# Eight dummy matmuls, a new order of the set-up block and one weight made by an accumulating transfer, in a causal convolution by nested differences

## Chip, cores, metric

The kernel runs on one core of one Trainium2 chip. The metric is the device time of one execution in microseconds (us). Before the change it was 780.17 us (median of three, 780.01 to 780.49). A ratio is the mean of a kernel's runs over the mean of the runs of before in the same rounds, so it is not quite the ratio of the medians that are quoted.

## The reference

A causal convolution of eight taps, each a 512 x 512 matrix:

```python
out = np.zeros_like(x)                      # x: 8 x 4096 x 512, kernel: 8 x 512 x 512
for k in range(8):
    shifted = x if k == 0 else np.concatenate([np.zeros((B, k, D)), x[:, :-k, :]], axis=1)
    out += np.matmul(shifted, kernel[k])
```

## The kernel before

Time is cut into 128 runs of 256 steps, one run to a partition, and eight steps make a group. Inside a group the eight taps are applied by three nested levels of a multiplication-saving scheme: sums of x (tiles `D4`, `D42`, `D421`, ...) meet 8 loaded weights and 19 differences of weights (index `MID`). A **node** is one third of a group: nine products of four 512-column matmuls each. The steady loop runs the nodes with TensorE gapless. What the change touches is the set-up block before it, in which the taps land, the first x is transposed by TensorE, node 0 is computed by 16 plain products (`direct`), and VectorE makes the 19 differences. Each engine runs its own instructions in the order of the text; waits between engines follow from the tiles they share.

```python
def fill(pw):                                # a pair of dummy matmuls on zeros
    for h in range(2):
        nc.tensor.matmul(pw[:, h], lhsT=zero[:, 0:P], rhs=zero, start=True, stop=True)

def product(bank, comp, w, start):           # four 128x512 matmuls
    for c in range(DC):
        nc.tensor.matmul(bank, lhsT=comp[:, c * P:(c + 1) * P], rhs=w[:, c, :], ...)

def mid_dve(*which):                         # one weight difference on VectorE
    o, u, v = mid(*which)
    tt(o, u, v, SUB)

def node_a1(k):  ...  # product into q[:, 1]; ScalarE copies it to q[:, 0]
def node_a0(n):       # product onto q[:, 0]
def node_u(n):        # product onto q[:, 1]: must wait for that copy
def node_seed(n, b_): # ScalarE copies q[:, 1] to the bank where the node's v product adds
def node_dts(n):      # ScalarE copies q[:, 0] to SBUF
def node_d(n, b_):    # VectorE: correction from dts and v
# ... cut ...
    direct(3, 0)
    fill(pair(2))
    direct(3, 1)
    tt(D41[:, 1], T4[:, 0], T4[:, 1], ADD)
    load_w(3)
    node_a1(1)
    node_u(nodes[1])
# ... cut ...
    node_a0(nodes[3])
    node_e(nodes[2], 0)
    prep_d42(HI)
    node_l(nodes[2], 1, LO)
    node_u(nodes[3])
    node_seed(nodes[3], 0)
    node_l(nodes[2], 1, HI)
    mid_dve(0, HI, LO)
    node_seed(nodes[3], 1)
```

## Time and profile before

| | before |
|---|---|
| span of the profiled execution | 778.4 us |
| TensorE busy | 765.6 us, 98% |
| VectorE busy | 658.7 us, 85% |
| first product starts | 11.78 us |
| x transposes (first work that needs the second load of x) start | 24.51 us |
| TensorE gapless from | 60.67 us |
| TensorE's waits from 24.5 to 61 us, summed | 2.8 us |

Read such a profile from its end: the chain that ended last says which engine set each stretch. The share of busy time hides that the first 61 us and the rest have different limits. A matmul's own line gives the idle time before it in brackets, and what ended it; for a wait that a pipelined engine can hide in its queue, the distance from start to start is the better measure, 216 ns where nothing waits.

### The profile page before, as it was taken

To read this page: it belongs to the slowest core of one execution; us is meant where nothing else is said; L and a number is where in the kernel's file an instruction comes from. 1 tells how busy PE (TensorE), PEld (TensorE's weight loads), DVE (VectorE), ACT (ScalarE), POOL (GpSimd) and SP (SyncE) were. 2 spreads that over 40 slices of the span, in tenths; PEclk is the share of its full clock that TensorE was granted. 3 is DMA by queue.
4 is the path that set the end of the run, shared out by engine and by line. 5 is a ranking of instruction groups with operands and counts; after the bars stand their busy time and mean duration, and the time that the engine had idled before them with its cause. 6 is when DMAs were issued, how large, how long until landed. Compare 5 with 4: busy or idle time off the path is not lost.

```text
span 778.4 us, 9432 instructions
## 1 busy us (share of the span) xinstructions
PE 765.6 (98%) x3576; PEld 346.9 (45%) x3576; DVE 658.7 (85%) x767; ACT 282.7 (36%) x461; POOL 41.2 (5%) x79
## 2 busy tenths in 40 slices
PE   6999999999999999999999999999999999999997
PEld 3444444444444444444444444444444444444443
DVE  4999988898888898888898888898888898878895
ACT  3453343333343333343333343333343333343332
POOL 4000000000000000000000000000000000000000
PEclk9999999999999999999999999999999999999999
DMA  9975887877787878787787687877797867687843
GB/s 198 211 125 137 214 198 181 194 166 185 166 177 194 195 166 177 171 194 179 175 189 183 166 202 170 195 168 185 166 192 176 204 162 185 167 181 184 205 132 122
DMA packets 159229, 138.90 MB, mean 178 GB/s; under 512 B 130128, under 2 KB 134224, under 8 KB 159056
## 3 DMA queue, kind: packets, MB, share of 16 engines
q1 hardware_dynamic: 145456, 99.89, 46.0%
q0 software_dynamic: 13584, 38.15, 31.1%
q8 instruction: 28, 0.46, 0.2%
q10 hardware_dynamic: 144, 0.26, 0.1%
q14 instruction: 17, 0.14, 0.1%
HBM read 77.33 MB, written 67.11 MB: 186 GB/s over the span
## 4 chain that ended last, share of the span: by engine, by line
PE 92%; DVE 4%; DMA 2%; issue 1%; POOL 1%; DVEq 0%; ACT 0%; ACTq 0%; POOLq 0%
PE pp L190 92%; DMA xin<-in_x_dram 2%; DVE w L76 2%; DVE D L76 1%; POOL w L80 0%; DVE pp L76 0%; DVE pp L265 0%; DVE XT L383 0%; PE pp L179 0%; DVE y L76 0%; DVE A L76 0%; POOL xin L80 0%; DVEq L635 0%; ACT pp L249 0%; POOL XT L80 0%
## 5 line engine op out<-in xcount | busy, mean ns | idle before, releaser
L190 PE MATMUL pp<-w,D 128*128 128x512 bf16 x3280 | 716.8, 379 | 4.2 <-DMA w<-in_kernel_dram 2.6
L190 PEld LDWEIGHTS <-D 128*128 128x128 bf16 x3280 | 320.4, 98 | 392.8 <-issue 3.3
L76 DVE TENSOR_TENSOR D<-D 128x1024 bf16<-128x1024 bf16 (+1 forms) x252 | 228.4, 945 | 1.0 <-ACT D L346 0.9
L76 DVE TENSOR_TENSOR y<-pp,ms 128x1024 f32<-128x1024 f32 (+1 forms) x121 | 146.2, 1211 | 45.4 <-PE pp L190 45.4
L76 DVE TENSOR_TENSOR D<-XT 128x2048 bf16<-128x2048 bf16 (+2 forms) x153 | 142.3, 945 | 11.2 <-DMA XT<-xin 9.2
L237 ACT COPY pp<-pp 128x512 f32<-128x512 f32 x95 | 54.1, 570 | 255.1 <-PE pp L190 255.0
L249 ACT COPY pp<-pp 128x512 f32<-128x512 f32 x95 | 54.2, 570 | 172.2 <-PE pp L190 170.0
L76 DVE TENSOR_TENSOR pp<-dts,pp 128x512 f32<-128x512 f32 x95 | 65.5, 689 | 43.9 <-ACT dts L255 42.6
L292 ACT COPY ms<-pp 128x1024 f32<-128x1024 f32 x60 | 61.0, 1016 | 33.0 <-PE pp L190 33.0
L80 POOL DMA_DIRECT2D xin<-in_x_dram x64 | 34.0, 532 | 687.2 <-DMA XT<-xin 672.6
L265 DVE SCALAR_TENSOR_TENSOR pp<-pp,dts 128x512 f32<-128x512 f32 x95 | 65.8, 693 | 3.3
L255 ACT COPY dts<-pp 128x512 f32<-128x512 f32 x95 | 57.5, 606 | 2.0 <-PE pp L190 2.0
L251 ACT ACTIVATE pp<-pp 128x512 f32<-128x512 f32 x95 | 56.1, 590 | 0.8 <-DVE y L76 0.8
L190 PE MATMUL pp<-w,XT 128*128 128x512 bf16 x120 | 30.8, 379 | 0.0
L76 DVE TENSOR_TENSOR w<-w,w 128x2048 bf16<-128x2048 bf16 x19 | 22.8, 1217 | 0.3 <-DMA w<-in_kernel_dram 0.2
L190 PEld LDWEIGHTS <-XT 128*128 128x128 bf16 x120 | 11.7, 98 | 14.2
L190 PE MATMUL pp<-w,w 128*128 128x512 bf16 x36 | 9.2, 378 | 1.3 <-ACT pp L237 0.7
L190 PE MATMUL pp<-w,F 128*128 128x512 bf16 x36 | 8.9, 379 | 0.0
L391 ACT COPY XT<-pp 128x1024 bf16<-128x1024 bf16 x1 | 1.0, 1012 | 17.5 <-PE pp L179 17.5
L173 PE MATMUL pp<-zero 128*128 128x512 bf16 x16 | 6.1, 539 | 1.2 <-DVE zero L145 1.2
L331 DVE MEMSET D<- 128x64 bf16 x2 | 0.2, 112 | 7.9 <-ACT D L343 7.7
L80 POOL DMA_DIRECT2D w<-in_kernel_dram x8 | 6.0, 755 | 4.1 <-DMA w<-in_kernel_dram 3.0
(53 smaller groups left out, 69.9 us busy)
## 6 DMA issues: line engine op xcount, KB each, us to landing
out_dram<-y SPq DMA_DIRECT2D x123, 512.0 KB, 3.5
xin<-in_x_dram POOLq DMA_DIRECT2D x64, 512.0 KB, 5.8
w<-in_kernel_dram POOLq DMA_DIRECT2D x8, 512.0 KB, 17.5
D<-in_x_dram SPq DMA_DIRECT2D x1, 1024.0 KB, 4.9
out_dram<-ms SPq DMA_DIRECT2D x2, 512.0 KB, 3.2
out_dram<-f SPq DMA_DIRECT2D x2, 512.0 KB, 4.3
XT<-xin SPq DMA_TRANSPOSE x61, 6.1
XT<-in_x_dram POOLq DMA_DIRECT2D x1, 384.0 KB, 10.9
```

What stands on the lines that cost most here:

```text
L76: nc.vector.tensor_tensor(out=o, in0=a, in1=b, op=op)
L80: nc.gpsimd.dma_start(out=out, in_=src)
L173: nc.tensor.matmul(pw[:, h], lhsT=zero[:, 0:P], rhs=zero, start=True, stop=True)
L190: nc.tensor.matmul(bank, lhsT=comp[:, c * P:(c + 1) * P], rhs=w[:, c, :], start=start and c == 0, stop=c == DC - 1, skip_group_check=True)
L237: nc.scalar.copy(out=n.q[:, 0], in_=n.q[:, 1])
L249: nc.scalar.copy(out=n.p[b_][:, 1], in_=n.q[:, 1])
L251: nc.scalar.mul(out=n.p[b_][:, 1], in_=n.q[:, 1], mul=-1.0)
L255: nc.scalar.copy(out=n.dts, in_=n.q[:, 0])
L265: nc.vector.scalar_tensor_tensor(out=p[:, 0], in0=p[:, 1], scalar=-1.0, in1=n.dts, op0=MUL, op1=SUB)
L292: nc.scalar.copy(out=ms[b_], in_=p)
L331: nc.vector.memset(z[:, :, 0:D:G], 0.0)
L391: nc.scalar.copy(out=XT[:, 0:2], in_=bank["x2"][:, 0:2])
```

## The change

Its stated intent: keep TensorE's clock up while the first tap is on its way, fit the order of the set-up to measured landings, and take one weight difference off VectorE: ScalarE writes the negated weight and a transfer adds the other one to it.

```diff
+    def mid_neg(u, v):
+        nc.scalar.mul(out=W[MID, u, v], in_=W[LO, u, v], mul=-1.0)
+
+    def mid_acc(u, v):
+        nc.gpsimd.dma_start(out=W[MID, u, v], in_=W[HI, u, v], accum_op=ADD)
 ...
     transpose_pe("h1", 0, H, 6, 8)
+    fill(pair(2))
     nc.scalar.copy(out=to(XF[:, 0:2]), in_=prev(bank["h0"]))
-    first_run(XF[:, 0:2])
     transpose_pe("x0", 2, xin[0, 0], 0, 2)
     nc.scalar.copy(out=XF[:, 4:6], in_=bank["x0"])
+    nc.scalar.copy(out=to(XF[:, 2:4]), in_=prev(bank["h1"]))
+    fill(pair(2))
+    first_run(XF[:, 0:2])
     tt(D4[:, 0:2], XF[:, 0:2], XF[:, 4:6], ADD)
+    fill(pair(2))
     load_w(5)
-    transpose_pe("xb", 3, xin[0, 0], 2, 4)
+    transpose_pe("xb", 0, xin[0, 0], 2, 4)
 ...
     tt(D2, XF[:, 1:6], XF[:, 3:8], ADD)
+    fill(pair(2))
 ...
     mid_dve(2, LO, MID)
+    mid_neg(HI, LO)
 ...
     prep_d421(HI)
-    mid_dve(0, HI, HI)
+    mid_acc(HI, LO)
 ...
     node_a0(nodes[3])
+    tt(D21[:, 0:2], C0[:, 0:2], C1[:, 0:2], ADD)
+    node_u(nodes[3])
     node_e(nodes[2], 0)
     prep_d42(HI)
+    mid_dve(0, LO, HI)
     node_l(nodes[2], 1, LO)
-    node_u(nodes[3])
     node_seed(nodes[3], 0)
     node_l(nodes[2], 1, HI)
-    mid_dve(0, HI, LO)
     node_seed(nodes[3], 1)
-    tt(D421[:, 0:4], D42[:, 3:7], D42[:, 4:8], ADD)
+    node_dts(nodes[3])
+    node_v(nodes[3], 1)
 ... (lines are left out within the hunks too; some sixty more move by a few places. The operations added or removed are the four `fill`s, the negation and the transfer, and `mid_dve(0, HI, LO)`; `xb` changes its bank; everything else that stands here with one sign moves)
```

More of the change, by code (lines that the diff above doesn't have):

```diff
@@ L342 @@
     transpose_pe("h1", 0, H, 6, 8)
+    fill(pair(2))
     nc.scalar.copy(out=to(XF[:, 0:2]), in_=prev(bank["h0"]))
-    first_run(XF[:, 0:2])
     transpose_pe("x0", 2, xin[0, 0], 0, 2)
     nc.scalar.copy(out=XF[:, 4:6], in_=bank["x0"])
+    nc.scalar.copy(out=to(XF[:, 2:4]), in_=prev(bank["h1"]))
+    fill(pair(2))
+    first_run(XF[:, 0:2])
     tt(D4[:, 0:2], XF[:, 0:2], XF[:, 4:6], ADD)
+    fill(pair(2))
     load_w(5)
-    transpose_pe("xb", 3, xin[0, 0], 2, 4)
-    nc.scalar.copy(out=to(XF[:, 2:4]), in_=prev(bank["h1"]))
-    direct(0, 0)
-    nc.vector.tensor_copy(out=XF[:, 6:8], in_=bank["xb"])
+    transpose_pe("xb", 0, xin[0, 0], 2, 4)
     first_run(XF[:, 2:4])
     fill(pair(3))
+    direct(0, 0)
     transpose_pe("he", 1, H, 1, 4)
-    tt(D4[:, 2:4], XF[:, 2:4], XF[:, 6:8], ADD)
     load_w(7)
     load_x(0, 1)
+    nc.vector.tensor_copy(out=XF[:, 6:8], in_=bank["xb"])
     tt(D2, XF[:, 1:6], XF[:, 3:8], ADD)
+    fill(pair(2))
+    tt(D4[:, 2:4], XF[:, 2:4], XF[:, 6:8], ADD)
+    load_x(1, 0)
     direct(0, 2)
+    tt(to(E4[:, 1:4]), prev(bank["he"]), to(XF[:, 1:4]), ADD)
+    load_w(2)
+    direct(2, 2)
     direct(0, 3)
-    load_x(1, 0)
-    tt(to(E4[:, 1:4]), prev(bank["he"]), to(XF[:, 1:4]), ADD)
-    direct(2, 2)
+    direct(0, 1)
     nc.vector.tensor_copy(out=F0, in_=XF[:, 4])
-    direct(0, 1)
-    first_run(E4[:, 1:4])
     direct(1, 1)
@@ L370 @@
     mid_dve(1, LO, HI)
+    first_run(E4[:, 1:4])
     mid_dve(2, LO, HI)
+    load_w(0)
+    direct(2, 0)
     tt(F21, D2[:, 0:4], D2[:, 1:5], ADD)
-    direct(2, 0)
+    direct(2, 3)
     mid_dve(2, LO, LO)
-    load_w(2)
     mid_dve(1, LO, LO)
-    load_w(0)
     direct(1, 3)
-    direct(2, 3)
     mid_dve(2, LO, MID)
+    mid_neg(HI, LO)
     direct(1, 0)
@@ L385 @@
     direct(1, 2)
+    nc.scalar.copy(out=C0[:, 0:2], in_=XT[:, 6:8])
+    prep_d42(HI)
     tt(D42[:, 3], D4[:, 1], D4[:, 3], ADD)
@@ L393 @@
     nc.scalar.copy(out=XT[:, 2:4], in_=bank["x2"][:, 2:4])
-    nc.scalar.copy(out=C0[:, 0:2], in_=XT[:, 6:8])
     nc.scalar.copy(out=C1, in_=XT[:, 0:4])
-    prep_d42(HI)
     tt(T4, XT[:, 4:8], XT[:, 0:4], ADD)
     direct(3, 0)
-    fill(pair(2))
     direct(3, 1)
     tt(D41[:, 1], T4[:, 0], T4[:, 1], ADD)
-    load_w(3)
+    fill(pair(2))
     node_a1(1)
-    node_u(nodes[1])
     tt(D41[:, 0], D4[:, 7], T4[:, 0], ADD)
     tt(T42[:, 0:2], D4[:, 6:8], T4[:, 0:2], ADD)
+    load_w(3)
     tt(D421[:, 0], D42[:, 7], T42[:, 0], ADD)
@@ L409 @@
     mid_dve(1, HI, HI)
-    load_w(1)
+    node_u(nodes[1])
     node_e(nodes[0], 0)
-    load_x(1, 1)
-    load_x(2, 0)
     prep_d27()
     mid_dve(2, HI, LO)
+    load_w(1)
     node_a0(nodes[1])
+    load_x(1, 1)
     node_seed(nodes[1], 0)
@@ L419 @@
     node_dts(nodes[1])
+    load_x(2, 0)
     tt(D421[:, 1:4], T42[:, 0:3], T42[:, 1:4], ADD)
+    load_x(2, 1)
     node_d(nodes[1], 0)
@@ L423 @@
     mid_dve(1, HI, LO)
+    node_v(nodes[1], 1)
+    mid_dve(2, HI, HI)
+    mid_dve(2, HI, MID)
     node_e(nodes[0], 1)
-    mid_dve(2, HI, HI)
-    node_v(nodes[1], 1)
-    mid_dve(2, HI, MID)
     node_l(nodes[1], 0, HI)
-    load_x(2, 1)
     node_d(nodes[1], 1)
     prep_d421(HI)
-    mid_dve(0, HI, HI)
+    mid_acc(HI, LO)
     node_a1(2)
@@ L435 @@
     node_e(nodes[1], 0)
+    mid_dve(0, HI, HI)
     transpose_x(1, 1)
@@ L438 @@
     node_u(nodes[2])
+    prep_d4(HI)
     node_l(nodes[1], 1, LO)
-    node_seed(nodes[2], 0)
-    prep_d4(HI)
     nc.scalar.copy(out=D4[:, 2:4], in_=T4[:, 2:4])
@@ L444 @@
     node_seed(nodes[2], 1)
+    node_seed(nodes[2], 0)
     node_dts(nodes[2])
     node_v(nodes[2], 0)
+    node_e(nodes[1], 1)
     node_d(nodes[2], 0)
-    node_e(nodes[1], 1)
     node_v(nodes[2], 1)
-    node_l(nodes[2], 0, HI)
     nc.scalar.copy(out=D42[:, 3], in_=T42[:, 3])
@@ L454 @@
     nc.scalar.copy(out=U1, in_=XT[:, 0])
+    node_l(nodes[2], 0, HI)
     node_a1(3)
@@ L458 @@
     node_a0(nodes[3])
+    tt(D21[:, 0:2], C0[:, 0:2], C1[:, 0:2], ADD)
+    node_u(nodes[3])
     node_e(nodes[2], 0)
     prep_d42(HI)
+    mid_dve(0, LO, HI)
     node_l(nodes[2], 1, LO)
-    node_u(nodes[3])
     node_seed(nodes[3], 0)
     node_l(nodes[2], 1, HI)
-    mid_dve(0, HI, LO)
     node_seed(nodes[3], 1)
-    tt(D421[:, 0:4], D42[:, 3:7], D42[:, 4:8], ADD)
+    node_dts(nodes[3])
+    node_v(nodes[3], 1)
     node_e(nodes[2], 1)
-    node_dts(nodes[3])
-    mid_dve(0, LO, HI)
-    node_v(nodes[3], 1)
     tt(A1[:, 0], C0[:, 1], C1[:, 0], ADD)
     mid_dve(1, MID, HI)
+    tt(D421[:, 0:4], D42[:, 3:7], D42[:, 4:8], ADD)
     node_v(nodes[3], 0)
@@ L481 @@
     node_a0(nodes[4])
-    node_l(nodes[3], 0, HI)
     node_dts(nodes[4])
@@ L486 @@
     tt(A1[:, 1], C1[:, 0], C1[:, 1], ADD)
-    load_x(3, 0)
-    tt(D21[:, 0:2], C0[:, 0:2], C1[:, 0:2], ADD)
     transpose_x(2, 0)
     mid_dve(2, MID, LO)
+    node_l(nodes[3], 0, HI)
     node_e(nodes[3], 0)
@@ L496 @@
     node_seed(nodes[4], 1)
+    node_e(nodes[3], 1)
     node_v(nodes[4], 0)
-    node_e(nodes[3], 1)
     node_d(nodes[4], 0)
+    node_v(nodes[4], 1)
     node_a1(5)
-    node_v(nodes[4], 1)
     node_l(nodes[4], 0, HI)
@@ L505 @@
     prep_m()
-    node_a0(nodes[5])
-    node_seed(nodes[5], 0)
     node_d(nodes[4], 1)
     node_y(nodes[4], 0, LO)
+    node_l(nodes[4], 1, LO)
     tt(F21[:, 0], D2[:, 0], D21[:, 0], ADD)
     node_y(nodes[4], 0, HI)
-    node_l(nodes[4], 1, LO)
+    node_a0(nodes[5])
+    load_x(3, 0)
     prep_d4(LO)
+    node_seed(nodes[5], 0)
     node_l(nodes[4], 1, HI)
@@ L516 @@
     node_v(nodes[5], 0)
-    store(0, LO, 0, first[0, LO, 0])
+    prep_d27()
     node_seed(nodes[5], 1)
     node_y(nodes[4], 1, LO)
-    prep_d27()
     node_d(nodes[5], 0)
     node_v(nodes[5], 1)
+    node_a1(6)
+    tt(F21[:, 1], D21[:, 0], D21[:, 1], ADD)
+    store(0, LO, 0, first[0, LO, 0])
     node_d(nodes[5], 1)
     store(0, HI, 0, first[0, HI, 0])
-    tt(F21[:, 1], D21[:, 0], D21[:, 1], ADD)
+    load_x(3, 1)
     node_y(nodes[4], 1, HI)
-    node_a1(6)
     node_l(nodes[5], 0, LO)
     node_a0(nodes[6])
-    load_x(3, 1)
     transpose_x(2, 1)
@@ L536 @@
     prep_d41(LO)
-    node_y(nodes[5], 0, HI)
+    node_l(nodes[5], 1, HI)
     node_l(nodes[5], 1, LO)
@@ L540 @@
     store(0, HI, 1, first[0, HI, 1])
+    node_y(nodes[5], 0, HI)
     node_y(nodes[5], 0, LO)
+    node_seed(nodes[6], 1)
+    tt(D21[:, 0:2], D2[:, 0:2], D2[:, 1:3], ADD)
     node_v(nodes[6], 0)
-    node_l(nodes[5], 1, HI)
+    node_y(nodes[5], 1, HI)
+    node_dts(nodes[6])
     store(1, LO, 0, first[1, LO, 0])
-    node_dts(nodes[6])
+    node_d(nodes[6], 0)
+    node_y(nodes[5], 1, LO)
+    node_v(nodes[6], 1)
+    node_d(nodes[6], 1)
     store(1, HI, 0, first[1, HI, 0])
-    tt(D21[:, 0:2], D2[:, 0:2], D2[:, 1:3], ADD)
-    node_d(nodes[6], 0)
-    node_y(nodes[5], 1, HI)
-    node_y(nodes[5], 1, LO)
-    node_seed(nodes[6], 1)
-    node_v(nodes[6], 1)
     tt(D21[:, 2:4], D2[:, 2:4], D2[:, 3:5], ADD)
-    node_d(nodes[6], 1)
     prep_d42(LO)
     store(1, HI, 1, first[1, HI, 1])
-    node_a1(7)
     prep_d4(HI)
     store(1, LO, 1, first[1, LO, 1])
+    node_a1(7)
     for k, (i, a) in enumerate(order):
```

## The prediction

> **What bounds the kernel now.** I read the page's busy table first, then the chain that ended last, then a table of stretches, then each engine's timeline of the first 62 us.
>
> ```profile
> PE 765.6 (98%) x3576; PEld 346.9 (45%) x3576; DVE 658.7 (85%) x767; ACT 282.7 (36%) x461; POOL 41.2 (5%) x79
> ...
> PE pp L190 92%; DMA xin<-in_x_dram 2%; DVE w L76 2%; DVE D L76 1%; POOL w L80 0%; DVE pp L76 0%; DVE pp L265 0%; DVE XT L383 0%; PE pp L179 0%; DVE y L76 0%; DVE A L76 0%; POOL xin L80 0%; DVEq L635 0%; ACT pp L249 0%; POOL XT L80 0%
> ```
>
> TensorE is the bound: 98% busy, 92% of the chain. The source has 16 products in the set-up block and 9 for each of 95 nodes, 871 in all, each of four 512-column matmuls: 3484. Their median spacing in the trace is 216 ns, so they need 3484 x 0.216 = 752.5 us of the 778.4 us span. No part of the change removes one. What it can win is time in which TensorE waits before it becomes gapless. When is that?
>
> ```profile
> 5.94 18.53 DMA xin<-in_x_dram
> ...
> 24.51 1.08 PE pp L179 x16
> ...
> 59.39 1.24 DVE w L76
> 60.63 0.05 issue
> 60.67 169.66 PE pp L190 x784
> ```
>
> This is the chain in order of time (start, us, what). It has three parts: until 24.46 us it waits for a load of x, queued since 5.94 us; from 25.6 to 60.6 us it runs through VectorE without a break; from 60.67 us TensorE is gapless. Everything the change touches is in the first two parts, and 717 us of the span are out of its reach.
>
> ```profile
> 8.30:11.70 3.40, 0.92 (x17) 0.74 (x14) 1.76 (x5) 2.17 (x3) 1.29 (x2) 0.97 1.17 197
> 11.70:15.10 3.40, 3.32 (x16) 1.68 (x17) 1.84 (x2) 0.00 (x0) 1.49 (x2) 0.53 1.12 186
> ...
> 15.20:18.50 3.30, 2.25 (x14) 1.06 (x12) 2.99 (x5) 0.00 (x0) 0.74 (x1) 1.00 1.23 201
> ```
>
> The stretches' columns are length, busy time of TensorE, its weight loads, VectorE, ScalarE and GpSimd, the granted clock, the DMA share and GB/s. TensorE works 0.92 us in the first stretch, and in the next its clock is 0.53. That is what the dummy matmuls are to cure.
>
> The remaining waits, from TensorE's timeline:
>
> ```profile
> 11.78 1.87 PE L190 MATMUL pp<-w,D 128*128 128x512 bf16 x4 [2.56 <-DMA w<-in_kernel_dram]
> ...
> 16.47 4.48 PE L190 MATMUL pp<-w,D 128*128 128x512 bf16 x20 [1.05 <-DVE w L76]
> ...
> 33.63 1.02 PE L190 MATMUL pp<-w,w 128*128 128x512 bf16 x4 [0.66 <-ACT pp L237]
> ...
> 36.18 2.02 PE L190 MATMUL pp<-w,w 128*128 128x512 bf16 x8 [0.66 <-ACT pp L249]
> ...
> 52.63 6.27 PE L190 MATMUL pp<-w,D 128*128 128x512 bf16 x28 [0.35 <-ACT pp L251]
> ```
>
> I measured each wait as the start-to-start distance of neighbours less 0.216 us. After 24.5 us: 0.82 at 33.63, 0.82 at 36.18, 0.13 at 37.17, 0.23 at 46.06, 0.51 at 52.63, 0.05 at 54.41, 0.21 at 60.67. Sum 2.8 us. All later ones add to about 0.5 us. So even a perfect set-up after 24.5 us would win 2.8 us, 0.4% of the time.
>
> **What the Trainium skill says.** (1) "TensorE: Matmul & The Clock Gate", Part 1: an idle array falls to half clock, judged in free-running windows of 3.4 us. The trace agrees: 3.4 us at about half clock after the nearly idle stretch, with 427 ns between matmuls (12.16 to 12.59 us) in place of 216. (2) Same page, Part 4: transposes do not count as busy in the same way. The trace fits: the 17 transposes in the first stretch did not hold the clock; it does not separate this from plain idleness. (3) "DMA: Bandwidth & Descriptors", section "SWDGE vs HWDGE vs iDMA": an accumulating transfer can only be issued by GpSimd, so the new one shares that queue with the x loads. (4) Same page, "Two DMAs through the same engine are not ordered": a queue's transfers start in order. The trace's landings agree: the loads issued between 1.9 and 28.5 us land in order of issue, mostly 2.5 us apart (taps 4, 6, 5, 7 at 11.64, 16.13, 18.67, 21.22; x at 24.46 and 26.56; taps 2, 0, 3, 1 at 29.10, 31.64, 34.19, 36.74; x at 39.18 and 41.66).
>
> **Part 1: dummy matmuls and the new order before 24.5 us.** The change adds four pairs of dummies (8 matmuls, 8 x 0.216 = 1.7 us warm). Three pairs stand before the first product, one before the second; all in time that was idle or cold. I walked the new order by hand. ScalarE's first three copies stay about 1 us each but the middle two shift, VectorE copies x's second half at about 11.8 (0.7 us), and the first product now also waits for that copy because it takes over its PSUM bank: start about 12.6, later than 11.78, but warm, so it ends near 13.5 as before. The H transposes (landing 13.54) end near 14.3; VectorE does the 5-row and 2-row adds, then the add into E4 ends near 15.6, which frees the bank for the second product: 15.6 against 16.47. Nine products follow, 9 x 0.864 = 7.8 us, ending at 23.4 against 24.24. The next work in both orders is the transposes of the x that lands at 24.46, and the same ten products stand before it in both. **The 0.9 us gained is therefore waited away there.** The order of loads is the same in both, and the queue never runs dry, so the landing stays. Worth: 0.0; only an execution with a badly placed clock window (0.27 us of slack in before) could show more.
>
> **Part 2: 24.5 to 38 us.** The same products, transposes and one dummy pair stand in the same order (the pair moves behind one product). The two 0.82 us waits are a product that must wait for ScalarE to read the bank it will write; the order around both is unchanged. Worth: 0.
>
> **Part 3: the weight made by DMA, and the order from 38 to 61 us.** ScalarE negates one weight (2048 columns; a copy of that size took 1.91 us) in time when it idles, so that is free. VectorE loses one 1.22 us subtraction, 1.14 us of its pitch, which stood at 49.39 us. A 1,024-column add moved ahead of the third node's gives 0.60 back until 56 us:
>
> ```profile
> 51.51 0.57 ACT L249 COPY pp<-pp 128x512 f32<-128x512 f32 x1 [1.64 <-PE pp L190]
> 51.99 0.59 ACT L251 ACTIVATE pp<-pp 128x512 f32<-128x512 f32 x1
> ...
> 54.27 0.69 DVE L265 SCALAR_TENSOR_TENSOR pp<-pp,dts 128x512 f32<-128x512 f32 x1
> ```
>
> The 0.51 us wait at 52.63 is a product waiting for these two ScalarE seeds, which wait for the product before. That product (the u of node 3) moves one place earlier, so two products (1.73 us) cover the 1.1 us of seeds in place of one: the wait goes. Then VectorE must keep up: its correction of node 3 moves from 54.27 to 54.27 - 1.14 + 0.60 = 53.7 and ends at 54.4, for a product at 54.7; the last two mid weights end 1.1 us earlier, near 59.4 and 60.5, for products near 59.9 and 60.8. The 0.21 goes too. The 0.23 at 46.06 stays, since the VectorE operations ahead of it are the same and one waits for a transposed x (landed 43.74). Sum: 0.51 + 0.21 + 0.05 = **0.75 us**.
>
> **Rivals.** (a) **The accumulating transfer lands late.** It is issued after the x load that went out at 44.26, so about 45; that load's data ended near 48.7 and landed at 50.97. Estimate for the add: 2.5 to 3 us of data like a load, then a landing up to 2.3 us after, so 52 to 54. The subtraction that reads it now stands at 55.47 - 1.14 + 0.60 = 54.9 in VectorE's order, and its result is needed near 56.4. A landing at 57 would cost 57 + 1.2 - 56.4 = 1.8 us: the kernel would take about 781.2. For it: no transfer of this kind is in the trace, and transposes use the engines from 49 to 52.6 us. Against it: the order is said to be fitted to measured landings. I give it a third. (b) **The warm clock is worth its face value**: the 3.4 cold us bring 1 us or more, and the result is near 778.5. For it: the cold stretch is real. Against it: the 24.46 landing. (c) **New waits** in the reordered nodes 4 to 6, where before had none: up to 0.5 us slower, 780.3.
>
> **Range and chances.** 780.17 - 0.75 = 779.4 with the transfer in time; a third of a chance of something like +0.3 us from it moves the middle to 779.5. The low end takes rival (b) in full, the high end a transfer about 1.5 us too late. The executions of before spread by 0.48 us, which is inside the range. All of it is far inside 2% (15.6 us): 98 to 99% within, 1% faster, under 1% slower.
>
> **What would show it.** In the changed profile: the granted clock near 1.0 from 11.7 to 15.1 us (the dummies did their work), the second product about 0.9 us earlier, and yet the x transposes still starting within 0.1 us of 24.5; the waits near 33.6 and 36.2 still there with 0.66; the one near 52.6 gone; VectorE without a wait for a DMA near 55 us; TensorE's gapless part starting with the same work about 0.7 us earlier. The prediction is wrong if the x transposes start well before 24.4, if a load lands at another time, or if VectorE waits for the accumulated weight.

## The result, and the profile after

779.5 us (median of four, 779.29 to 779.61) against 780.09 us for before in the same rounds: ratio 0.9992, 95% interval 0.9974 to 1.0009. By this interval it is "the same". All four executions lie below all four of before, and in the second measurement (below) four of five lie below all nine, so a small gain is likely; how large it is, the times don't settle. The traces can say more, because they show each wait.

The page of the changed kernel, busy time and chain by line:

```profile
PE 766.8 (99%) x3584; PEld 347.3 (45%) x3584; DVE 657.5 (85%) x766; ACT 284.9 (37%) x462; POOL 42.3 (5%) x80
...
PE pp L197 96%; DMA xin<-in_x_dram 2%; POOL w L80 0%; PE pp L186 0%; ACT y L295 0%; DVE y L76 0%; DVE pp L76 0%; POOL xin L80 0%; DVEq L647 0%; ACT pp L256 0%; ACT pp L244 0%; POOL XT L80 0%; PE pp L180 0%; POOL ident masks.py:199 0%; POOL ident masks.py:197 0%
```

The eight dummies make TensorE look 1.2 us busier, and the span is 1.1 us shorter all the same: busy time of a dummy is not work. VectorE has one instruction less. Its lines of weights have left the chain, and TensorE's share rose from 92 to 96%. The chain in order of time:

```profile
5.96 18.30 DMA xin<-in_x_dram
...
24.31 1.07 PE pp L186 x16
...
45.14 0.69 DVE pp L76
45.83 0.04 issue
45.87 726.95 PE pp L197 x3364
```

It still waits for the same load of x, landed at 24.26 us (24.46 before). But the 35 us through VectorE are gone from it: VectorE still has as much to do, but its last step on this chain is the correction that ends at 45.83 us. The stretches, columns as in the prediction:

```profile
8.30:11.70 3.40, 2.19 (x17) 1.04 (x15) 0.83 (x3) 2.20 (x3) 0.00 (x0) 1.00 1.17 193
11.70:15.10 3.40, 3.05 (x29) 1.71 (x27) 2.89 (x5) 0.00 (x0) 2.57 (x4) 1.00 1.15 187
...
15.20:18.50 3.30, 2.49 (x12) 1.20 (x13) 2.92 (x6) 0.09 (x1) 0.86 (x2) 1.00 1.23 203
```

The clock is 1.00 where it was 0.53. One trace doesn't show that the dummies did it, since windows fall differently in each execution; but over all profiles, none of the six with the added dummies has a cold (half-clock) window between 8 and 30 us, and six of the eight without them have one or two (most of these versions are described below). TensorE's timeline, start and length in us, idle time before in brackets:

```profile
13.01 1.02 PE L197 MATMUL pp<-w,D 128*128 128x512 bf16 x4 [0.35 <-DVE D L367]
...
16.01 4.48 PE L197 MATMUL pp<-w,D 128*128 128x512 bf16 x20 [0.88 <-DVE w L76]
...
24.31 1.07 PE L186 MATMUL pp<-ident,xin 128*128 128x128 bf16 x16 [0.37 <-DMA xin<-in_x_dram]
...
33.44 1.02 PE L197 MATMUL pp<-w,w 128*128 128x512 bf16 x4 [0.66 <-ACT pp L244]
...
35.98 2.02 PE L197 MATMUL pp<-w,w 128*128 128x512 bf16 x8 [0.66 <-ACT pp L256]
37.87 20.26 PE L197 MATMUL pp<-w,D 128*128 128x512 bf16 x92
```

The second product starts 0.46 us earlier, and then the x transposes wait for their load. The two waits of 0.66 us are where they were. From 37.87 us on 92 matmuls follow with no wait in the listing where before had one at 52.63 us.

The account of the 1.08 us by which the last matmul starts earlier (772.43 against 773.51 us): the load of x landed 0.20 us earlier; the waits from 24.3 to 62 us sum to 2.2 in place of 2.8 us (0.78 to 0.14 between 50 and 62 us); the small waits after 62 us sum to about 0.25 us less. Only the middle item, 0.6 us, is the change's by the argument of the prediction. The medians differ by 0.59 us.

One measure takes out the landing of x: the time from the start of the x transposes to the start of the last matmul. It is 749.00 to 749.45 us in six profiles with the old order (before, and the variants of it below) and 748.02 to 748.65 us in six with the new order (the changed kernel twice, its variants without dummies, and the short load). The two groups do not overlap, though single late waits of 0.3 to 0.7 us stand in both.

### The profile page after: what moved, and what is told of

Its sections match the earlier page's. It is cut to its first block, busy times and chain, and to the rows that moved or that the text cites. A ratio compares the mean times of both kernels' runs of the same rounds, so it can differ in the third digit from the quotient of the medians.

```text
span 777.3 us, 9450 instructions
## 1 busy us (share of the span) xinstructions
PE 766.8 (99%) x3584; PEld 347.3 (45%) x3584; DVE 657.5 (85%) x766; ACT 284.9 (37%) x462; POOL 42.3 (5%) x80
## 4 chain that ended last, share of the span: by engine, by line
PE 96%; DMA 2%; POOL 1%; ACT 0%; issue 0%; DVE 0%; DVEq 0%; POOLq 0%
PE pp L197 96%; DMA xin<-in_x_dram 2%; POOL w L80 0%; PE pp L186 0%; ACT y L295 0%; DVE y L76 0%; DVE pp L76 0%; POOL xin L80 0%; DVEq L647 0%; ACT pp L256 0%; ACT pp L244 0%; POOL XT L80 0%; PE pp L180 0%; POOL ident masks.py:199 0%; POOL ident masks.py:197 0%
## 5 line engine op out<-in xcount | busy, mean ns | idle before, releaser
L180 PE MATMUL pp<-zero 128*128 128x512 bf16 x24 | 8.9, 505 | 2.4 <-DVE zero L145 1.2
L197 PEld LDWEIGHTS <-w 128*128 128x128 bf16 x36 | 3.5, 97 | 5.8 <-issue 2.1
```

## The experiments

My theory: the load of x that lands near 24.3 us sets the start of what follows, so nothing done before it counts; the gain is that ScalarE's seeds of node 3 and VectorE's last weights no longer make TensorE wait between 50 and 62 us, and both had to go together. Rivals: the warm clock is worth its face value; or VectorE's saved subtraction is.

### The dummies alone

To the kernel before I added the four pairs only, at the same places (after the `h1` transposes, two after the copy of `x0`, one after the add into `D2`).

> The kernel before with nothing but the four added pairs of dummy matmuls. My theory (the x load that lands near 24.3 to 24.5 us sets the start of everything after it): the clock stays near 1.0 from 11.7 to 15.1 us, the second product starts about 1 us earlier (near 15.4 in place of 16.47), TensorE then idles about 1.3 us before the x transposes, which still start within 0.05 us of that load's landing; time within 0.2 us of before, so 780.0 to 780.3. Rival (the warm clock is worth its face value): about 1 us faster, near 779.1.

Measured: 781.05 us against 780.48 us, ratio 1.0004 (0.9992 to 1.0017): no gain. The median is above the 780.0 to 780.3 that I had said: the profiled execution took 780.48 us, the four others 780.83 to 781.17, and no trace shows why. From the stretches and TensorE's timeline of this run:

```profile
11.70:15.10 3.40, 2.85 (x27) 1.71 (x26) 2.74 (x4) 0.00 (x0) 2.68 (x4) 1.00 1.14 192
```

```profile
16.19 4.48 PE L190 MATMUL pp<-w,D 128*128 128x512 bf16 x20 [1.58 <-DVE w L76]
...
24.49 0.68 PE L179 MATMUL pp<-ident,xin 128*128 128x128 bf16 x9 [0.38 <-DMA xin<-in_x_dram]
```

The clock is full, and the x transposes start at 24.49 us, where the load landed at 24.45. My figure for the second product was wrong: 16.19, not 15.4, because in the old text order the dummies wait for a ScalarE copy and hold up the transposes behind them. It made no difference, which is the point. The waits from 24.5 to 62 us equal those of before. The rival's 1 us is not there.

### The changed kernel without the dummies

> The changed kernel without the four added pairs of dummies, its order kept. My theory: the clock falls to a half somewhere between 11.7 and 16 us, the first product and the H transposes run at half rate, the second product starts near 16.8 in place of 16.01, the ten products end near 24.6 in place of 23.6, so at most 0.3 us of it passes the load's landing at 24.3: 779.5 to 779.8. Rival (warm clock worth its face value): 1 us or more slower than the changed kernel, 780.5 or above.

Measured: 780.18 us against 780.48 us for before, ratio 0.9997 (0.9983 to 1.0010). In its trace one clock window is cold (from 12.0 to 15.4 us), the second product starts at 16.20, the x transposes at 24.37 with the load landed at 24.32, and the waits to 62 us sum to 2.07 us: the set-up is as good as with the dummies. But TensorE waited 0.67 us near 386 us, far from anything changed. The median stood above my range; that wait explains it for the profiled execution alone. I ran the kernel again, below.

### The u product alone, the transfer alone, both

The first variant of before:

```diff
     node_a0(nodes[3])
+    node_u(nodes[3])
     node_e(nodes[2], 0)
     prep_d42(HI)
     node_l(nodes[2], 1, LO)
-    node_u(nodes[3])
```

> The kernel before with only the u product of node 3 moved one place earlier, which in the changed kernel covers the two ScalarE seeds. My theory: the 0.51 us wait near 52.6 goes, but VectorE, whose list is unchanged and without a gap to 60.6 us, does not get earlier, so TensorE waits about as long a little later (near 54.7 for the correction of node 3 that ends at 54.96, and near 60.7 for the mid weight): gapless part starts at 60.67 as before; time 780.0 to 780.2. Rival (the wait is worth its own length wherever it is removed): 0.5 us faster, 779.6.

The second replaces `mid_dve(0, HI, LO)` in before by `mid_neg` and `mid_acc`, at the changed kernel's places:

> The kernel before with only the weight by negation and accumulating transfer in place of one VectorE subtraction. My theory: VectorE is about 1.1 us earlier from 49.4 us on, waits up to 0.6 us for the transfer (landing near 54.9 as in the changed kernel), the 0.51 us wait near 52.6 stays because ScalarE's seeds make it, the 0.21 us at 60.67 goes: 0.2 to 0.3 us faster, 779.8 to 779.9. Rival (the freed 1.14 us of VectorE is worth itself): 1.1 us faster, 779.0.

The third does both:

> The kernel before with both: the u product of node 3 one place earlier and the weight by negation and accumulating transfer. My theory (the two waits guard one another: ScalarE's seeds at 52.6 us, VectorE's list from 54 to 60.7 us): the waits between 50 and 62 us, 0.78 us in before, 0.78 with the first part alone and 0.55 with the second alone, fall to 0.1 to 0.2 us, so 0.6 to 0.7 us faster than before, which is the whole gain of the changed kernel without its dummies and without its new front. Rival (effects add): 0 plus 0.23 us, so 0.55 us of waits stay.

| kernel | median us | before us | ratio (95% interval) | waits in its trace, 50 to 62 us |
|---|---|---|---|---|
| before | | | | 0.52 + 0.05 + 0.21 = 0.78 us |
| u product alone | 780.15 | 780.48 | 0.9999 (0.9986 to 1.0011) | 0.57 + 0.21 = 0.78 |
| transfer alone | 780.36 | 780.48 | 1.0002 (0.9989 to 1.0014) | 0.51 + 0.04 = 0.55 |
| both | 780.59 | 780.60 | 1.0005 (0.9992 to 1.0017) | 0.35 |
| changed kernel | 779.50 | 780.09 | 0.9992 (0.9974 to 1.0009) | 0.14 |

None of the four ratios is clear of 1, and the times of the transfer alone and of both missed what I had said (779.8 to 779.9, and 0.6 to 0.7 us faster). The waits are read from one profile each; before's 0.78 us came out the same in the profiles of the dummies alone and of the short load. The waits of the first two are as expected: moving the product alone moves the wait 2 us on, to a product that needs a weight from VectorE (I had expected it to wait for the correction):

```profile
55.26 4.49 PE L190 MATMUL pp<-w,D 128*128 128x512 bf16 x19 [0.40 <-DVE w L76]
```

(That execution runs 0.9 us late, see the next part, so 55.26 is 54.4 of before.) The two together take out 0.43 us, where I had said 0.6 to 0.7. What is left shows in VectorE's timelines, the first line from the kernel with both, the second with the transfer alone:

```profile
54.33 0.70 DVE L271 SCALAR_TENSOR_TENSOR pp<-pp,dts 128x512 f32<-128x512 f32 x1 [0.44 <-ACT dts L261]
```

```profile
54.14 0.70 DVE L271 SCALAR_TENSOR_TENSOR pp<-pp,dts 128x512 f32<-128x512 f32 x1 [0.61 <-ACT dts L261]
```

VectorE now waits for node 3's `dts`, a ScalarE copy that stands behind a 1 us copy of node 2's result in the old order. The changed kernel puts it ahead of that copy (the last `+` lines of the diff above), which I had not counted as a part of its own. So the two together are not the whole gain. That `dts` is the **third** part is argued and not tested by a run of its own: the changed kernel also moves a 1,024-column add (0.60 us of VectorE) out of this stretch, which might cover the 0.35 us by itself.

The time of the variant with both shows none of its 0.43 us: its load of x landed at 24.95, 0.5 us later than before's, and it had the 0.7 us wait near 387 us too (the transfer alone had 0.58 us there). Executions differ by as much as the whole gain.

### What the clock costs when it falls for longer

The profile of the u product alone happened to fall on an execution with two cold windows in a row (12.7 to 19.5 us); from its stretches and its TensorE timeline:

```profile
12.70:19.50 6.80, 5.23 (x22) 2.62 (x22) 5.05 (x7) 0.00 (x0) 1.48 (x2) 0.50 1.23 203
```

```profile
25.38 1.06 PE L179 MATMUL pp<-ident,xin 128*128 128x128 bf16 x16
```

The load had landed at 24.35 us, yet the transposes start at 25.38, right behind the product before: here TensorE itself is late. This execution has a mean clock of 0.994. This kernel's two executions at 0.994 took 781.10 and 780.93 us, its three at 1.0 took 780.06 to 780.15: two cold windows cost 0.9 us. One alone costs nothing (before's own profile has one, and its x transposes start 0.05 us after the landing), so this is the price of the second. Over all runs with the old beginning (before and its variants without the added dummies), 6 of 46 executions of which I have the clock were at 0.994. With the dummies (the changed kernel twice, and the short load below) none of 13 was under 0.999. If the dummies prevent it, they are worth 0.9 us in one execution in eight, about 0.1 us in the mean, and nothing in the median. That it is they is not shown: the 15 executions of the new order without dummies (below) had none at 0.994 either, the lowest being one at 0.995. The prediction had this only as a half sentence ("an execution with a badly placed clock window").

### Taking the landing away

Both kernels with a quarter of tap 7 loaded and the rest zeros, so that the x load behind it lands earlier. Their outputs are wrong, which doesn't matter for the times.

```diff
-    load_w(7)
+    w7 = W[LO, LO, LO]
+    load(w7[:, 0:1], kr[:, 0:1, 7, :])
+    for c in range(1, DC):
+        nc.scalar.copy(out=w7[:, c], in_=zero)
```

> Wrong result on purpose: the kernel before, but only a quarter of tap 7 is loaded (the rest is zeros written by ScalarE), so that the load of x behind it lands about 1.9 us earlier, near 22.5 us. My theory: TensorE reaches the x transposes when its ten products are done, near 24.25 us, in place of 24.5, so they start at most 0.3 us earlier and the time falls by 0.2 to 0.3 us; in an execution whose clock falls to a half for two windows nothing is won. Rival (the landing isn't what binds): no change in both kernels.

> Wrong result on purpose: the changed kernel with the same quarter of tap 7. My theory: its ten products are done near 23.6 us, so the x transposes now start near 23.6 in place of 24.3 and the time falls by about 0.7 us against the changed kernel; the part of the front's gain that the landing hid comes out. Rival (the landing isn't what binds): no change.

The load landed at 22.12 us in the one and 21.62 us in the other. The x transposes, in before and in the changed kernel:

```profile
23.36 1.06 PE L179 MATMUL pp<-ident,xin 128*128 128x128 bf16 x16
```

```profile
23.75 1.06 PE L186 MATMUL pp<-ident,xin 128*128 128x128 bf16 x16
```

Now nothing waits for the load, and both start right behind their ten products: 1.15 us earlier in the variant of before, 0.56 us in that of the changed kernel. Times: 779.59 us for the first (three executions at 779.54 to 779.62, one at a clock of 0.994 at 781.20) and 778.77 us for the second, against 780.60 us for before: ratios 0.9994 (0.9980 to 1.0008) and 0.9980 (0.9964 to 0.9995), the second alone clear of 1. The theory that this landing binds holds by the traces, and the times agree: with it out of the way both kernels gain about 1 and 0.7 to 0.8 us (the second against the changed kernel's 779.5, from other rounds). That before gained more than I had said has a plain reason: this profile fell on an execution with no cold window at all, so its products, from 11.36 us on, ran warm. The old beginning with a warm clock is in fact 0.4 us quicker through its ten products than the new one, whose first product waits for a VectorE copy until 13.01 us; only the landing hides it. (The profile of the transfer alone, warm by chance too, shows the same: second product at 15.34 us, where the changed kernel has 16.01.) In its one execution with a double cold window the same kernel lost 1.6 us rather than 0.9, presumably since no landing is left to hide any of it.

### Why a kernel without dummies waited near 386 us

A DMA transpose of x landed late there. The trace's transfers show a fetch of 16 KB by the instruction queue inside it (28 such packets in a run, one for each 256 of TensorE's some 7,150 instructions, so I take them to be TensorE's). The eight dummies with their weight loads are 16 instructions, and in the profiles with dummies that fetch came some 5 us earlier. Over the whole of before's trace, the 13 DMA transposes in which such a fetch started between issue and landing took 7.2 us in the mean, the 48 others 5.7 us; a slow transpose has more time to meet a fetch, so this alone does not say which causes which. To separate this from warmth I added 16 instructions that warm nothing to the kernel without dummies, and ran it beside the changed kernel and the kernel without dummies, both unchanged.

```diff
     for k in range(6):
         fill(pair(k % 4))
+    for _ in range(4):
+        pw = pair(2)
+        for h in range(2):
+            nc.tensor.matmul(pw[:, h, 0:4], lhsT=zero[:, 0:P], rhs=zero[:, 0:4], start=True, stop=True)
```

> The changed kernel again, beside its own variants on one chip. Expected: no execution with a mean clock under 0.998, 779.2 to 779.8 us, 0.7 to 1.0 us under the mean of before, whose executions spread over 1 us because some have two cold windows.

> The changed kernel without the four added pairs of dummies, again. In its first profile the waits of the set-up were the same as the changed kernel's, but TensorE waited 0.67 us near 386 us, behind a DMA transpose that landed 7.4 us after its issue, with a fetch of instructions for TensorE at 380.9 in between; in the profiles with dummies that fetch came 5 us earlier, and the transpose took 5.7 us. Theory (the dummies act also by where the 16 added instructions move the fetches): 779.9 to 780.3 as before, the wait near 386 again. Rival (chance): the wait is not there this time and the time is that of the changed kernel in executions without a double cold window.

> The same without the dummies, but with 8 matmuls of 4 columns (and so 8 weight loads) right after the first dummies, where TensorE waits for x anyway: the same 16 instructions are added, but they keep nothing warm. Fetch theory: the instruction fetch moves back to near 375 us, the transpose takes about 5.7 us again, no wait near 386: about 0.6 us faster than the kernel without dummies in executions with at most one cold window, so as the changed kernel (779.3 to 779.7), while a double cold window still costs 0.5 to 0.9 us. Rival (only the warm clock matters): the time of the kernel without dummies, 780.0 or more, wait near 386 still there.

Measured, before on this chip at 780.19 us: changed kernel 779.56 (ratio 0.9991, 0.9977 to 1.0005), without dummies 779.56 (0.9992, 0.9979 to 1.0004), with the 16 small instructions 779.42 (0.9987, 0.9975 to 1.0000). VectorE's add that waits for the transpose, first without dummies, then with the small instructions:

```profile
382.72 1.23 DVE L76 TENSOR_TENSOR D<-XT 128x2048 bf16<-128x2048 bf16 x1 [1.75 <-DMA XT<-xin]
```

```profile
381.69 1.22 DVE L76 TENSOR_TENSOR D<-XT 128x2048 bf16<-128x2048 bf16 x1 [0.82 <-DMA XT<-xin]
```

The fetch moved from 380.6 to 375.5 us and the transpose took 5.8 us in place of 6.7. All profiles but those of the two attempts below agree that the place of the fetch goes with the length of that transfer. In the seven without the 16 added instructions the fetch came at 380.4 to 382.4 us and the transpose took 6.7 to 7.5 us, in the five with them 374.8 to 376.8 us and 5.7 to 5.8 us. But this time VectorE's 1.75 us of waiting was still inside its slack; the first profile, at 2.46 us, passed it on to TensorE, as did those of the transfer alone and of both (2.37 and 2.49 us). So of the four profiles with the transfer and without the 16 instructions three show that wait, and none with the instructions does; how often it comes is not known. In the times the rival is right: the kernel without dummies equals the changed one, 779.56 us both. None of the changed kernel's four, then five executions had a clock under 1.0, as expected; two took 779.88 and 780.08 us, above what I had said.

### Two attempts at a faster version

Two of the waits, 0.82 us each from start to start, are left in the changed kernel. The first attempt moved three differences to GpSimd, split adds so that node 1 can start earlier, and held two products back to cover those waits. Its core, on GpSimd:

```diff
+    def mid_pool(*which):
+        o, u, v = mid(*which)
+        nc.gpsimd.tensor_tensor(out=o, in0=u, in1=v, op=SUB)
 ...
+    mid_pool(0, LO, HI)
+    mid_pool(0, HI, HI)
+    mid_pool(0, HI, LO)
```

> A version meant to beat both: the changed kernel, but three of the weight differences are made by GpSimd, which idles from 29 to 44 us, in place of one by a transfer; the adds behind the second x load are cut in halves so that node 1 starts earlier; two of the set-up products are held back to cover the two 0.82 us waits. My theory: if one such difference takes GpSimd 4.7 us or less and does not slow VectorE, the waits from 24.3 to 62 us fall from about 2.1 us to under 0.7 us: 1.4 to 1.8 us faster than the changed kernel. Rival: GpSimd is slower than that or slows VectorE, and the new list of VectorE waits for it near 47 to 53 us: no gain or a loss of 1 us or more.

Correct, and 789.52 us (ratio 1.0116, 1.0102 to 1.0130): 9 us slower. GpSimd's timeline, then VectorE's:

```profile
29.12 12.69 POOL L167 TENSOR_TENSOR w<-w,w 128x2048 bf16<-128x2048 bf16 x3 [0.19 <-DMA w<-in_kernel_dram]
```

```profile
29.17 4.54 DVE L76 TENSOR_TENSOR w<-XT 128x1024 bf16<-128x1024 bf16 x1
33.75 4.15 DVE L76 TENSOR_TENSOR D<-w 128x512 bf16<-128x512 bf16 x1
37.82 4.27 DVE L76 TENSOR_TENSOR D<-D,w 128x512 bf16<-128x512 bf16 x1
```

GpSimd needs 4.2 us for one, as hoped. But a VectorE add of 512 columns, 0.42 us elsewhere, took 4.15 us beside it: for 12.7 us VectorE got through three adds. TensorE waited 7.4 us for them, and its clock stood at half from 33.6 to 43.8 us. The Trainium skill has this, in "SBUF — State Buffer", section "Who interferes with whom": VectorE's second input shares a port with GpSimd's reads, as an exclusive lock. The trace fits, each of the three adds lasting about as long as one of GpSimd's subtractions, and reading that page before the run would have saved it.

The second attempt left GpSimd alone, split the copy of the first transposed x between VectorE and ScalarE, kept the split adds and the held-back products, and issued the accumulating transfer before the last x load of the set-up.

> A second version meant to beat both: no work on GpSimd. Changed kernel, with the copy of the first transposed x shared by VectorE and ScalarE, the adds behind the second x cut in halves so that node 1 starts at about 30.2 in place of 31.75 us, two set-up products held back to cover the two 0.82 us waits, and the accumulating transfer issued before the last x load, at about 37 us. My theory: those two waits fall under 0.2 us, but VectorE, which sheds only 0.6 us, then sets the pace at 45 to 61 us: waits from 24.3 to 62 us of 0.9 to 1.4 us in place of 2.1, 0.6 to 1.1 us faster than the changed kernel. Rival: the transfer and the x transpose that both run at 39 to 45 us delay one another, and the gain is lost: within 0.3 us of the changed kernel or slower.

784.59 us (ratio 1.0049, 1.0036 to 1.0061), and its result was **wrong** (relative error 0.099). Worked through in the order of its text (a calculation, which no run on the chip shows), its arithmetic gives the reference's result, so the fault lies in something that overlaps, or in something I did not see; which stays open, and the time is used only for one reading. VectorE's and TensorE's timelines:

```profile
48.14 1.22 DVE L76 TENSOR_TENSOR D<-XT 128x2048 bf16<-128x2048 bf16 x1 [2.68 <-DMA XT<-xin]
```

```profile
50.15 10.50 PE L197 MATMUL pp<-w,D 128*128 128x512 bf16 x40 [2.83 <-DVE D L76]
```

The rival came true: the transfer (37.74 to 44.76 us) and the x transpose (issued 39.72) ran together, and the transpose landed at 48.12 us, 8.4 us after its issue, where it took 4.5 us in the changed kernel. TensorE waited 2.83 us for it, and then ran at half clock from 50.6 to 54.0 us. No version that I tried beats the changed kernel.

## Why the prediction was right

**The bound and its reach.** Right: TensorE's work is the same, and all that could be won was waits before 61 us.

**Part 1, the dummies and the front, worth 0.** Right in its sum: the clock went from 0.53 to 1.00 and the x transposes still start 0.05 us after their load (before with the dummies alone: the same; the changed kernel without them: the same time). Its inner times were off by 0.4 us: the first product at 13.01, not 12.6, the second at 16.01, not 15.6. The short load showed that the new beginning, with the landing out of the way, is not quicker than the old one on a warm clock. The slack of 0.27 us was named, but the double cold window, 0.9 us in 6 of 46 executions, was not weighed.

**Part 2, worth 0.** Right: both waits are there unchanged, 0.66 us in the listing.

**Part 3, 0.75 us** (its terms add to 0.77). Right in mechanism, and near in size: 0.64 us of waits less between 50 and 62 us in the profile, 0.53 in the second one. Two terms differ. The wait at 60.67 us did not go, it shrank from 0.21 to 0.14, because of rival (a). And the argument left out that `dts` moved up on ScalarE: the u product and the transfer by themselves give 0.43 us.

**Rival (a), the transfer too late.** It came within 0.1 us of the limit. I estimated a landing at 52 to 54 us and a need at 54.9; it landed at 54.86, and VectorE's subtraction started when it did:

```profile
54.15 0.68 DVE L76 TENSOR_TENSOR pp<-dts,pp 128x512 f32<-128x512 f32 x1
54.89 1.23 DVE L76 TENSOR_TENSOR w<-w,w 128x2048 bf16<-128x2048 bf16 x1
```

VectorE's pitch after such an instruction is 0.60 us elsewhere, so 0.14 us were lost here. In the second profile it landed at 55.08 us, and 0.21 us stayed at 60.9 us:

```profile
55.10 1.23 DVE L76 TENSOR_TENSOR w<-w,w 128x2048 bf16<-128x2048 bf16 x1 [0.17 <-DMA w<-w]
```

By the prediction's own sign ("wrong if VectorE waits for the accumulated weight") this step failed, by a tenth or two of a microsecond. The other profiles of the new order agree that this is all that was missing: where the transfer landed at 52.23 to 53.44 us (the first without dummies, the small instructions, the short load) VectorE did not wait, and no wait over 0.03 us was left between 50 and 62 us: the full 0.78 us; where it landed at 54.86 to 55.08 us, 0.14 to 0.31 us stayed. In the changed kernel's profile the x load ahead landed at 52.16 us, 7.8 us after its issue, in place of 6.7. Over all eight profiles with the transfer at this place, the transfer landed 8.7 to 8.9 us after its issue when issued by 44.72 us, and 9.8 to 10.2 us after when issued from 44.87 us on; why is open.

**Rival (b)**, face value of the clock: refuted by the dummies alone. **Rival (c)**, new waits: one of 0.13 us at 68.6 us, where before had one of 0.11 us at 71.2 us.

**The figure.** 779.5 us predicted and measured. That it agrees to the tenth is luck: executions of one kernel differ by 0.3 to 1 us (landing of the x load 24.26 to 24.95 us over the traces, late transposes, cold windows), and no ratio of the changed kernel to before excludes 1.

## What to carry to other kernels

Before judging what warms or shortens a beginning, find the transfer that the next stage waits for, and ask whether the same work stands before it in both versions; if so, the gain is waited away. When a wait is removed and its engine's neighbour runs without a gap, look one wait further: here the product's move alone won nothing, the transfer alone 0.23 us of waits, both 0.43 us, and the whole new order 0.5 to 0.8 us. Where the effect is under the spread of executions, count waits in the traces and use the clock of each execution to sort them; do not read a story from the medians.

## What the Trainium skill lacked or had wrong

- "TensorE: Matmul & The Clock Gate", Part 1: agrees in its windows of 3.4 us, and it says that the cold start varies with their placing. That such a window's cost can vanish behind a late load, in whole or in part, it does not say: the same old beginning had 0, 1 or 2 cold windows in different executions, the first cost nothing behind a late load, and the second 0.9 us.
- "DMA: Bandwidth & Descriptors", section "SWDGE vs HWDGE vs iDMA": names accumulation as GpSimd's, with no rate. Measured for 512 KB from SBUF to SBUF: 0.89 us of GpSimd to issue, landing 2.7 us after the x load ahead of it, 9.9 us after issue (8.7 to 10.2 us over eight profiles); a DMA transpose beside it took 11.3 us against a median of 6.1 in that run, and 8.4 against 4.5 us in the second attempt.
- "Runtime: NRT & Kernel Launch", section "Instruction fetch mechanics": calls the cost of a fetch at a block's boundary mostly hidden. That is so for the engine that fetches (after 62 us TensorE's waits in the changed kernel sum to some 0.2 us, through most of its 28 fetches), but DMA transposes with a fetch between issue and landing took 7.2 us against 5.7 in before's trace (a difference that longer transposes can in part make by themselves), and 16 added instructions moved one such fetch by 5 us and shortened the transpose around it from 6.7 to 5.8 us.
- "SBUF — State Buffer", section "Who interferes with whom": right; what it costs here is 4.15 us in place of 0.42 for a VectorE add of 512 columns.
